# HGRN2 mixer of a four-stage encoder trunk: the value projection as one seven-product 2x2 block product behind four plain gate chunks

## The chip, the cores and the metric

The kernel runs on one core of one Trainium2 chip. The metric is the device time of one execution in microseconds (us); a few executions are taken and their median is given. One more execution is recorded with the hardware profiler, and every row of a profile below comes from such a recording. Time inside the recording is counted from the start of its span.

## What is computed

Two token batches (512 and 256 tokens, 768 in all, 1024 features) go through two macaron layers with shared weights. The first layer's mixer is the one that changes:

```python
# x = x + 0.5 * swiglu_ffn(rmsnorm(x))        for each layer, then the mixer, then a second ffn
def hgrn2_mixer(x, w_in, w_o, g_norm, lb):
    q, i, g, f_fw, f_bw = jnp.split(x @ w_in, 5, axis=-1)     # w_in: [1024, 5*1024]
    f = lb + (1 - lb) * sigmoid(fpre);  k = 1 - f             # per direction
    # S_t = diag(f_t) S_{t-1} + k_t v_t^T,  o_t = S_t^T q_t   forward and backward, v = i
    o = rmsnorm_per_head(o_fwd + o_bwd) * g_norm
    return (o * silu(g)) @ w_o
```

`w_in` has five column ranges of 1024: q, the values i (called v below), g, and the two gate inputs f. There are 8 heads of 128 columns.

## The kernel before, in words

Everything is f32, and each matrix product is taken in three passes on TensorE: every operand is split into a high part (`hi`, a cast to fp32r on ScalarE) and a low part (`lo`, the rest, a subtraction on VectorE), and hi*hi, hi*lo and lo*hi are accumulated in PSUM (`mm3`, L259 to L263). A weight tile needs one cast (L167 or L200 or L266) and one subtraction (L168, L201, L267) before it is used.

The program is written in Python and fully unrolled; a scheduler that ranks instructions by program order, data and free buffers sets the order on each engine. Each engine then runs its own instructions strictly in that order. Buffers come from rings: 8 split weight tiles (`w`), 4 raw weight tiles of 512 KB (`wr`), 2 small raw tiles (`s3`), 8 temporaries (`tA`), 21 large tiles of 6 KB per partition (`big`), 6 token tiles (`x`), 8 PSUM banks (`ps`).

Weights are planned in one queue (`plan`, `plan_quad`) in the order of use. `load_next` issues the DMAs of the next entry on SyncE's queue (SP) when raw tiles are free; `stage_next` splits it into `w` tiles; `take`, `done` and `ahead` keep at most 8 `w` tiles staged.

The feed-forward blocks already use a seven-product scheme: the 2x2 block product of (token halves x feature halves) with (feature halves x column halves) is made with 7 block products in place of 8. Its token factors are b00, b10, b01, b11 (feature half, token half; `block` and `put`) and four sums t1 to t4 of them (`mix`, `sums`, L364 to L379); its weight factors are sums of the four weight blocks, which are made partly by adding DMAs on GpSimd's queue (`into`, L141) and partly on VectorE (L207).

At the end of a feed-forward block, `after_block` normalizes each token block and queues `turn` as deferred work; `turn` (L318) transposes the normalized blocks on TensorE (L331) and copies them out of PSUM. For a feed-forward block the copies go to `tn` (f32) and are split by `put`. For a mixer (row 1 or 4) each copy is split straight out of PSUM into `self.h` (L345 on ScalarE, L346 on VectorE).

The mixer `hgrn` (L832) then runs, in this order: the first half of v's columns for all 768 tokens (`proj_tok("v0")`, 6 blocks of 128 tokens, 24 matmuls of 512 columns each, tokens as the stationary operand); head 0's q and f chunks (`hgrn_proj`, 3 chunks, each 24 matmuls over the 512 tokens and 24 over the 256 tokens, weights stationary); then for each head the scan (`hgrn_scan`, L695: 7 levels of small f32 matmuls at L693, with copies on ScalarE L723 and multiplications on VectorE L745, L749, L751 and predicated copies L712 between the levels), woven with the projection chunks of the next head. The second half of v (`proj_tok("v1")`) is woven into the scan of head 3. After the last scan come g and the output projection.

Of the kernel before, what the change touches and what calls it, by code (L numbers as in the profile page):

```python
# [9 lines left out]
F32 = mybir.dt.float32  # L10
F32R = mybir.dt.float32r
U8 = mybir.dt.uint8
AF = mybir.ActivationFunctionType
# [20 lines left out]
SEQS = ((0, TA), (TA, TB))  # L34
# [8 lines left out]
PACKED = 1  # L43
UP = ("p1", "p7", "p2", "p5", "p4", "p6", "p3")
DOWN = ("p1", "p2", "p5", "p4", "p7", "p6", "p3")
FACTOR = {"p1": "b00", "p2": "b10", "p3": "b11", "p4": "t4", "p5": "t1", "p6": "t2", "p7": "t3"}


class Trunk:
# [94 lines left out]
    def load_next(self):  # L144
        key, srcs, shape, how = self.queue.pop(0)
        raws = []
        for src in srcs:
# [25 lines left out]
    def quad_steps(self, key, raws, srcs, order):  # L173
# [43 lines left out]

        return [(1 if up else 2, lambda name=name: step(name)) for name in order]

    def stage_next(self):  # L220
# [97 lines left out]
    def turn(self, half, part, row, first=False):  # L318
        nc = self.nc
        feeds_ffn = row % 3 != 1  # L320
        if half == 0 and part == 0:
            if feeds_ffn:
                self.ops = {}
                self.tn = {}
            else:
                self.h = [self.big([P, 2, T], F32R) for _ in range(NC)]
# [277 lines left out]
    def proj_tok(self, tag, evac):  # L604
        rest = None
        for gb in range(NBLK):
# [3 lines left out]
            for k in range(NC):  # L610
                key = (tag, k // 2)
                wh, wl = self.take(key)
                a, c = (self.h[k][:, 0, sl], self.h[k][:, 1, sl]), (wh[:, k % 2, :], wl[:, k % 2, :])
                self.mm3(ps, a, c, k == 0, k == NC - 1)
# [43 lines left out]

    def hgrn_proj(self, h, out):
        nc = self.nc  # L660
        qk = self.big([P, 2, T])
        qs, kd = qk[:, 0, :], qk[:, 1, :]
        f, q, k = (self.big([P, 2, T]) for _ in range(3))
        for c0, dst, func in ((0, qs, AF.Copy), (3, f[:, 1, :], AF.Sigmoid), (4, f[:, 0, :], AF.Sigmoid)):
            key = ("hgrn", h, c0)
            wh, wl = self.take(key)
            for s, (off, n) in enumerate(SEQS):
                ps = self.ps(n)
                for kk in range(NC):
                    b = tuple(self.h[kk][:, i, off : off + n] for i in range(2))  # L670
                    self.mm3(ps, (wh[:, kk, :], wl[:, kk, :]), b, kk == 0, kk == NC - 1)
                    if kk in ((1, 3, 5), (3,))[s]:
                        yield
                nc.scalar.activation(dst[:, off : off + n], ps, func)
                if s:
                    self.done(key)
                yield
        for d in range(2):
# [4 lines left out]
        nc.vector.tensor_add(kd, k[:, 0, :], k[:, 1, :])  # L683
        out.update(h=h, qs=qs, kd=kd, f=f, q=q, k=k)

# [122 lines left out]
    def plan_hgrn(self, w_in, w_o):  # L808
        self.plan_tok("v0", w_in, D)
        for h in range(HEADS):  # L810
            for c in (0, 3, 4):
                lo = c * D + h * P
                self.plan(("hgrn", h, c), w_in[:, lo : lo + P], (NC, P))
            if h == 4:
                self.plan_tok("v1", w_in, D + 512)
# [16 lines left out]
    def hgrn(self, lb_row, gn_row, next_row):  # L832
        nc = self.nc
        with self.tc.issue_after(self.last_act), self.tc.issue_after(self.last_dve):
            self.lower_bounds(lb_row)
        self.load_masks()
        self.later(self.spill_x)
        self.hss = self.cp.tile([P, HEADS, NBLK], F32, name="hss")
        vs = {}

        def put_v(half):
            def f(s, b, ps):
                gb = SEQS[s][0] // P + b
                if gb not in vs:
                    vs[gb] = self.xt()
                nc.scalar.copy(vs[gb][:, half * 512 : (half + 1) * 512], ps)

            return f

        self.drain(self.proj_tok("v0", put_v(0)))  # L850
        scan = lambda hd: self.hgrn_scan(hd, vs)
        heads = [{} for _ in range(HEADS)]

        def stream():
            for h in range(1, HEADS):
                yield from self.hgrn_proj(h, heads[h])
                if h == 4:
                    yield from self.proj_tok("v1", put_v(1))

        feed = stream()  # L860
        self.drain(self.hgrn_proj(0, heads[0]))
        lead, early = 4, 2
        for _ in range(lead + early):
            next(feed)
# [453 lines left out]
```

## Time and profile before

| what | us |
|---|---|
| median of 3 runs (2799.24 to 2799.45) | 2799.41 |
| the profiled execution | 2799.13 |
| its span in the trace | 2797.3 |
| last part of the first feed-forward block and first transposes | about 485 to 505 |
| v0, then head 0's chunks | 505 to 576 |
| scans of heads 0 to 7 woven with projections | 576 to 905 |

In the rows below a group reads: line, engine, operation, tile written <- tiles read, shape, xcount, then busy time and mean ns of one, then the engine's idle time just before and who ended it. In timeline rows the two first numbers are start and duration in us; a bracket at the end is idle time before the instruction and what released it. PE is TensorE, PEld its weight loads, DVE VectorE, ACT ScalarE, POOL GpSimd, SP SyncE.

### The profile page before, as it was taken

Reading aid. Unit: us, or ns where it says so; the run is one execution under the profiler, and the core shown is the slowest. Engines: PE = TensorE matmul, PEld = TensorE weight load, DVE = VectorE, ACT = ScalarE, POOL = GpSimd, SP = SyncE. Lnnn points to the kernel's source line nnn. Section 1 sums busy time; section 2 is a strip of 40 time slices with the busy share of each in tenths; the row PEclk is TensorE's granted clock in tenths of the full one; section 3 lists DMA queues with packets and bytes.
Section 4 is the critical chain, followed back from the end, with each engine's and each line's share of the span. In section 5 each row is a group of like instructions: output and inputs, shape, how many; then the busy total and the mean of one; then the engine's idle time right before and its main releaser. Section 6 shows DMA issues by size and latency. Waiting matters only on the chain.

```text
span 2797.3 us, 40580 instructions
## 1 busy us (share of the span) xinstructions
PE 2772.5 (99%) x15225; PEld 2553.0 (91%) x15225; DVE 2159.4 (77%) x3760; ACT 1329.7 (48%) x2455; POOL 369.2 (13%) x402
## 2 busy tenths in 40 slices
PE   8999999999999999999999999999999999999998
PEld 8999999889899889999999999999988889999998
DVE  8788788477577658878878887887858878778877
ACT  7344443444344436444444644444458855444443
POOL 2111121000000001111111111111003211211111
PEclk9999999999999999999999999999999999999999
DMA  6554464311111133555454355545422123655543
GB/s 175 128 129 119 115 144 122 111 46 39 46 40 37 61 98 76 140 133 127 111 128 124 76 137 133 130 111 128 132 72 76 37 61 77 147 133 128 117 115 108
DMA packets 330101, 291.37 MB, mean 104 GB/s; under 512 B 11608, under 2 KB 257840, under 8 KB 329904
## 3 DMA queue, kind: packets, MB, share of 16 engines
q1 hardware_dynamic: 293920, 212.37, 26.1%
q0 software_dynamic: 31680, 62.93, 13.2%
q10 hardware_dynamic: 4304, 13.49, 1.4%
q8 instruction: 119, 1.95, 0.3%
q14 instruction: 78, 0.64, 0.1%
HBM read 216.39 MB, written 9.44 MB: 81 GB/s over the span
## 4 chain that ended last, share of the span: by engine, by line
PE 96%; DVE 2%; ACT 1%; DMA 0%; issue 0%; DVEq 0%; ACTq 0%; SPq 0%
PE ps L437 42%; PE ps L501 20%; PE ps L261 9%; PE ps L263 9%; PE ps L262 9%; PE ps L693 3%; PE ps L797 1%; PE ps L1180 1%; PE ps L773 1%; PE ps L331 1%; PE ps L1142 0%; PE ps L1143 0%; PE ps L1192 0%; PE ps L1193 0%; PE ps L943 0%; DVE x L523 0%
## 5 line engine op out<-in xcount | busy, mean ns | idle before, releaser
L437 PE MATMUL ps<-big,w 128*128 128x384 f32 x6720 | 1169.3, 334 | 0.0
L437 PEld LDWEIGHTS ps<-big,w 128*128 128x128 f32 x6720 | 1165.9, 188 | 1.7 <-ACT tA L454 0.2
L200 ACT CAST w<-wr 128x512 fp32r<-128x512 f32 x600 | 416.1, 706 | 683.5 <-PE ps L437 281.8
L501 PE MATMUL ps<-w,big 128*128 128x512 f32 x2520 | 575.6, 389 | 0.0
L501 PEld LDWEIGHTS ps<-w,big 128*128 128x128 f32 x2520 | 472.7, 188 | 97.8 <-DVE x L523 0.3
L201 DVE TENSOR_TENSOR w<-wr,w 128x512 fp32r<-128x512 f32 (+1 forms) x520 | 430.0, 831 | 155.1 <-ACT w L200 131.2
L523 DVE SCALAR_TENSOR_TENSOR x<-ps,x 128x512 f32<-128x512 f32 x468 | 301.3, 681 | 10.0 <-PE ps L263 9.9
L142 POOL DMA_DIRECT2D s<-wr x120 | 105.0, 875 | 1511.3 <-DMA wr<-in_ffn_w_dram 623.5
L261 PE MATMUL ps<-w,big 128*128 128x512 f32 x624 | 249.0, 399 | 0.5 <-DVE big L1203 0.2
L263 PE MATMUL ps<-w,big 128*128 128x512 f32 x624 | 244.8, 392 | 1.0 <-DVE big L346 1.0
L262 PE MATMUL ps<-w,big 128*128 128x512 f32 x624 | 244.0, 391 | 0.0
L261 PE MATMUL ps<-big,w 128*128 128x384 f32 (+2 forms) x640 | 220.1, 345 | 0.9 <-ACT w L167 0.8
L262 PE MATMUL ps<-big,w 128*128 128x384 f32 (+2 forms) x640 | 216.1, 338 | 0.3 <-DVE big L267 0.2
L263 PE MATMUL ps<-big,w 128*128 128x384 f32 (+2 forms) x640 | 215.2, 336 | 0.0
L266 ACT CAST big<-tA 128x384 fp32r<-128x384 f32 x296 | 148.0, 513 | 114.2 <-DVE tA L476 36.2
L267 DVE TENSOR_TENSOR big<-tA,big 128x384 fp32r<-128x384 f32 x296 | 167.4, 576 | 6.7 <-ACT big L266 4.5
L168 DVE TENSOR_TENSOR w<-wr,w 128x1024 fp32r<-128x1024 f32 x92 | 111.6, 1220 | 75.8 <-ACT w L167 70.4
L201 POOL TENSOR_TENSOR w<-wr,w 128x512 fp32r<-128x512 f32 x80 | 134.0, 1676 | 194.4 <-ACT w L200 193.6
L167 ACT CAST w<-wr 128x1024 fp32r<-128x1024 f32 x92 | 96.5, 1051 | 107.6 <-PE ps L262 85.7
L263 PEld LDWEIGHTS ps<-w,big 128*128 128x128 f32 x624 | 117.2, 188 | 27.1 <-DVE big L346 1.7
L142 POOL DMA_DIRECT2D wr<-wr x100 | 87.7, 877 | 410.5 <-DVE w L201 170.3
L261 PEld LDWEIGHTS ps<-w,big 128*128 128x128 f32 x624 | 117.3, 188 | 23.3 <-issue 1.0
(179 smaller groups left out, 3275.4 us busy)
## 6 DMA issues: line engine op xcount, KB each, us to landing
wr<-in_ffn_w_dram SPq DMA_DIRECT2D x264, 512.0 KB, 4.0
s<-in_ffn_w_dram SPq DMA_DIRECT2D x120, 256.0 KB, 3.3
s<-wr POOLq DMA_DIRECT2D x120, 256.0 KB, 4.9
wr<-wr POOLq DMA_DIRECT2D x80, 256.0 KB, 3.8
wr<-in_hg_w_in_dram SPq DMA_DIRECT2D x40, 512.0 KB, 3.8
wr<-wr POOLq DMA_DIRECT2D x20, 512.0 KB, 4.6
spill<-x ACTq DMA_DIRECT2D x12, 512.0 KB, 3.1
x<-spill ACTq DMA_DIRECT2D x12, 512.0 KB, 3.4
```

Source lines behind the costliest of these rows:

```text
L142: self.nc.gpsimd.dma_start(out, src, accum_op=ALU.add)
L168: self.nc.vector.tensor_sub(lo, raw, hi.bitcast(F32))
L200: nc.scalar.copy(h, src)
L201: (eng or nc.vector).tensor_sub(l, src, h.bitcast(F32))
L261: nc.tensor.matmul(out, a[0], b[0], start=first, stop=False)
L262: nc.tensor.matmul(out, a[0], b[1], start=False, stop=False)
L263: nc.tensor.matmul(out, a[1], b[0], start=False, stop=last)
L266: self.nc.scalar.copy(hi, src)
L267: self.nc.vector.tensor_sub(lo, src, hi.bitcast(F32))
L437: self.nc.tensor.matmul(ps, a[x], b[y], start=first and k == 0 and i == 0, stop=k == 3 and i == 2, skip_group_check=True,)
L501: nc.tensor.matmul(ps, a[x], w[y], start=name == chain and kp == 0 and q == 0, stop=kp == 1 and q == 2, skip_group_check=True,)
L523: self.nc.vector.scalar_tensor_tensor(x, ps, c, x, ALU.mult, ALU.add)
```

## The change

The v projection (both column halves) becomes one block product with 7 in place of 8 block multiplications, right at the start of the mixer but behind four plain chunks (`LEAD`: head 0's q, f forward, f backward, and head 1's q). The chunks are done by token halves of 384: all four for the first half of the tokens, then all four for the second half. The token factors are made as for a feed-forward block (`feeds_ffn = row != 4`), so `self.h` is gone for this mixer, and the projections read the factors b00 to b11. All later chunks are two passes of 384 tokens in place of 512 and 256. v1 is no longer woven into head 3's scan.

```diff
+TOK = ("p1", "p2", "p7", "p6", "p5", "p4", "p3")
+LEAD = ((0, 0), (0, 3), (0, 4), (1, 0))
...
+    def tok_steps(self, key, srcs):
...
+        def fetch(src):
+            t = self.wp.tile([P, 1024], F32, tag="wr", name=self.name("wr"), bufs=RAWBUFS)
+            nc.sync.dma_start(t.rearrange("p (a b) -> p a b", a=2), src[0])
+            parts = [[t], [self.tmp(512), self.tmp(512)]]
+            for a, t in enumerate(parts[1]):
+                self.last_load = nc.sync.dma_start(t, src[1][:, a, :])
+            return parts
+        a11, a12, a21, a22 = (fetch(src) for src in srcs)
+        more = self.big([P, 2, 512])
...
+        for kp in range(2):
+            for a, t in enumerate(s3[kp]):
+                self.last_load = nc.sync.dma_start(t, srcs[2][kp][:, a, :])
+                self.into(t, a11[0][0][:, a * 512 : (a + 1) * 512] if kp == 0 else a11[1][a])
+            for t, u in zip(a21[kp], a22[kp]):
+                self.into(t, u)
+        own = {"p1": a11, "p2": a12, "p3": a12, "p4": a22, "p5": a21, "p6": a11, "p7": s3}
+        sums = {"p6": (a11, a21), "p3": (a12, a11)}
...
-        feeds_ffn = row % 3 != 1
+        feeds_ffn = row != 4
...
-        if half and row % 3 != 1:
+        if half and row != 4:
             self.later(self.sums)
...
+    def tok_quad(self, key, tile):
...
+        for name in TOK:
+            ws = [self.take((*key, name, kp)) for kp in range(2)]
+            chain = {"p2": "p1", "p4": "p5", "p3": "p7"}.get(name, name)
+            for i in range(HB):
...
+                for k in range(4):
...
+                    for q, (x, y) in enumerate(((h, wh), (h, wl), (l, wh))):
+                        nc.tensor.matmul(
...
+                if name == "p1":
+                    nc.scalar.activation(x22, ps, AF.Copy, scale=-1.0)
+                elif name == "p2":
+                    nc.scalar.copy(x11, ps)
+                elif name == "p4":
+                    nc.vector.tensor_add(x21, ps, x22)
+                elif name == "p3":
+                    nc.vector.tensor_sub(x12, ps, x22)
+                elif name == "p5":
+                    nc.vector.tensor_sub(x22, x22, ps)
+                else:
+                    nc.vector.tensor_add(x22, ps, x22)
...
-        self.drain(self.proj_tok("v0", put_v(0)))
+        for half in range(2):
+            for n, (h, c) in enumerate(LEAD):
+                for i, _ in enumerate(self.hgrn_chunk(h, heads[h], c, (half,))):
+                    if half == 0 and n and i != 1:
+                        self.run_later()
+            self.run_later(len(self.deferred))
...
+        for name in self.tok_quad(("v",), vtile):
+            if name == "p6":
+                self.load_masks()
+                self.hgrn_gates(0, heads[0])
...
-            pieces = 18 + 24 * (h == 3) - (lead if h == HEADS - 2 else 0) - (early if h == 0 else 0)
+            pieces = 18 - (2 if h == 0 else 0) - (lead if h == HEADS - 2 else 0)
```

Where instructions stand now is shown at three places. In the rows that follow, numbers behind a name tell buffers apart, and the line is that of the program in question.

TensorE, behind the transposes of the first token half. Before, the first block of v follows: the moving operand (`w`, 512 weight columns) is listed first, the stationary one (`big`, tokens out of `self.h`) second.

```order
L331 MATMUL ps_4678<-ident_r,big_4522 128x128
L331 MATMUL ps_4678<-ident_r,big_4544 128x128
L261 MATMUL ps_4699<-w_4455,big_4594 128x512
L262 MATMUL ps_4699<-w_4456,big_4594 128x512
L263 MATMUL ps_4699<-w_4455,big_4594 128x512
L261 MATMUL ps_4699<-w_4455,big_4595 128x512
```

In the changed program, the same place on TensorE: two plain chunks (banks `ps_4724` and `ps_4751`, weights `w_4455` and `w_4476`, now the stationary operand) begin, with transposes of the second token half between them.

```order
L380 MATMUL ps_4701<-ident_r,big_4540 128x128
L309 MATMUL ps_4724<-big_4611,w_4455 128x384
L309 MATMUL ps_4751<-big_4611,w_4476 128x384
L380 MATMUL ps_4761<-ident_r,big_4562 128x128
L380 MATMUL ps_4761<-ident_r,big_4584 128x128
L380 MATMUL ps_4767<-ident_r,big_4562 128x128
L380 MATMUL ps_4767<-ident_r,big_4584 128x128
L310 MATMUL ps_4724<-big_4611,w_4455 128x384
L311 MATMUL ps_4724<-big_4611,w_4456 128x384
```

`big_4611` is the first half of the factor b00, which `put` writes out of `tn`. The order takes the 12 matmuls of both chunks on b00 before either goes on to b10.

VectorE, ahead of the first scan. Before, one weight of a later chunk (L168), the last gate of head 0 (L683) and the first level's multiplications (L751, L745, L749) stand ahead of the first copy of scores (L707):

```order
L168 TENSOR_TENSOR w_5113<-wr_4924,w_5112 128x1024
L680 TENSOR_SCALAR big_4941<-big_4941,lb_buf 128x768
L682 TENSOR_TENSOR big_4942<-big_4940,big_4941 128x768
L683 TENSOR_TENSOR big_4940<-big_4943 128x768
L751 TENSOR_TENSOR big_5188<-big_4941 128x2x384
L745 TENSOR_TENSOR big_4942<-big_4942,big_4941 128x2x384
L749 TENSOR_TENSOR big_4943<-big_4943,big_4941 128x384 x2
L168 TENSOR_TENSOR w_5182<-wr_4936,w_5181 128x1024
L707 COPY big_5187<-ps_5192 128x512
```

In the changed program the gates and the first level stand further ahead, beside p5 and p4, and right ahead of the first copy of scores (L810) come the weight sums (L255) and splits (L315) of the last product p3, the evacuations of p4 (L743) and p3 (L745), and four weights of later chunks (L173):

```order
L255 TENSOR_TENSOR wr_4645<-wr_4645,wr_4639 128x1024
L743 TENSOR_TENSOR x_5060<-ps_5276,x_5061 128x512
L315 TENSOR_TENSOR w_5320<-wr_4645,w_5319 128x1024
L255 TENSOR_TENSOR tA_4647<-tA_4647,tA_4641 128x512
L743 TENSOR_TENSOR x_5076<-ps_5290,x_5077 128x512
L315 TENSOR_TENSOR w_5326<-tA_4647,w_5325 128x512
L743 TENSOR_TENSOR x_5092<-ps_5304,x_5093 128x512
L745 TENSOR_TENSOR x_5077<-ps_5173,x_5077 128x512
L173 TENSOR_TENSOR w_5430<-wr_5335,w_5429 128x1024
L745 TENSOR_TENSOR x_5093<-ps_5187,x_5093 128x512
L173 TENSOR_TENSOR w_5436<-wr_5337,w_5435 128x1024
L810 COPY big_5441<-ps_5446 128x512
```

(Rows that only repeat one of these with another buffer are left out.) The splits of `w_5430` and `w_5436` need buffers of p3, so they wait for its end.

SyncE's DMA queue, from the first plain weight on. Before, plain weights of 512 KB alone stand there:

```order
L152 DMA wr_4332<-in_hg_w_in_dram 128x2x512
L152 DMA wr_4334<-in_hg_w_in_dram 128x2x512
L152 DMA wr_4378<-in_hg_w_in_dram 128x2x512
L152 DMA wr_4410<-in_hg_w_in_dram 128x2x512
L152 DMA wr_4459<-in_hg_w_in_dram 128x8x128
```

Now the four plain chunks come first, and v's four weight blocks follow, half in raw tiles and half in temporaries, with a third copy of one block (`big_4663`) between them:

```order
L157 DMA wr_4410<-in_hg_w_in_dram 128x8x128
L231 DMA wr_4639<-in_hg_w_in_dram 128x2x512
L234 DMA tA_4641<-in_hg_w_in_dram 128x512
L231 DMA wr_4645<-in_hg_w_in_dram 128x2x512
L234 DMA tA_4660<-in_hg_w_in_dram 128x512
L245 DMA big_4663<-in_hg_w_in_dram 128x512 x2
L231 DMA wr_4651<-in_hg_w_in_dram 128x2x512
L231 DMA wr_4657<-in_hg_w_in_dram 128x2x512
L191 DMA s_1276_8950<-in_ffn_w_dram 128x4x128
```

`wr_4639`, `wr_4645`, `wr_4651` and `wr_4657` are the first halves of the blocks a11, a12, a21 and a22. The program counts 14667 matmuls and transposes on TensorE before and 14631 now; the first 2648 and the last 10006 of them, that is all up to the end of the first feed-forward block and all from behind the last scan on, stand in the same order as before.

More of the change, by code (lines that the diff above doesn't have):

```diff
@@ new lines, in hgrn_chunk @@
+    def hgrn_chunk(self, h, hd, c0, halves):
+        key = ("hgrn", h, c0)
+        wh, wl = self.take(key)
+        if c0 == 0:
+            if "qk" not in hd:
+                hd["qk"] = self.big([P, 2, T])
+            dst, func = hd["qk"][:, 0, :], AF.Copy
+        else:
+            if "f" not in hd:
+                hd["f"] = self.big([P, 2, T])
+            dst, func = hd["f"][:, 4 - c0, :], AF.Sigmoid
+        for half in halves:
+            ps = self.ps(H)
+            for kk in range(NC):
+                b = self.operand(f"b{kk // 4}{half}", kk % 4)
+                self.mm3(ps, (wh[:, kk, :], wl[:, kk, :]), b, kk == 0, kk == NC - 1)
+                if kk in (2, 5):
+                    yield
+            self.nc.scalar.activation(dst[:, half * H : (half + 1) * H], ps, func)
+            if half:
+                self.done(key)
+            yield
@@ L678, in hgrn_proj, with hgrn_gates @@
+    def hgrn_gates(self, h, hd):
+        nc = self.nc
+        qs, kd, f = hd["qk"][:, 0, :], hd["qk"][:, 1, :], hd["f"]
+        q, k = (self.big([P, 2, T]) for _ in range(2))
         for d in range(2):
@@ L683, in hgrn_proj @@
         nc.vector.tensor_add(kd, k[:, 0, :], k[:, 1, :])
-        out.update(h=h, qs=qs, kd=kd, f=f, q=q, k=k)
+        hd.update(h=h, qs=qs, kd=kd, q=q, k=k)
     def halves(self, t, l, par, d):
```

111 lines of the change are left out of this document (70 added, 41 removed).

## The prediction

> **What bounds the kernel now.** First the page: the span, the busy shares, and the shares of the chain of work that ended last.
>
> ```profile
> span 2797.3 us, 40580 instructions
> PE 2772.5 (99%) x15225; PEld 2553.0 (91%) x15225; DVE 2159.4 (77%) x3760; ACT 1329.7 (48%) x2455; POOL 369.2 (13%) x402
> PE 96%; DVE 2%; ACT 1%; DMA 0%; issue 0%; DVEq 0%; ACTq 0%; SPq 0%
> ```
>
> The chain is TensorE, almost throughout. A busy TensorE need not be at its best pace, so the second view is what TensorE waited for in the mixer (485 to 910 us):
>
> ```profile
> PE ps L693 <- ACT big L723: 1.4, 1, 1.4
> PE ps L263 <- DVE big L346: 0.5, 1, 0.5
> ```
>
> Two waits, 1.9 us in 425: the mixer is a stream of matmuls with no hole worth filling. A change here is worth what it does to the number of matmuls times their pace, plus new waits, minus at most these 1.9 us.
>
> The pace is not the mean duration of a group, since matmuls overlap. It is read from the chain in order of time (start, us, what), where a piece ends as the next one starts:
>
> ```profile
> 428.06 28.60 PE ps L501 x126
> 456.66 29.14 PE ps L437 x168
> 615.82 2.68 PE ps L693 x24
> ```
>
> L501 has 512 columns, so 28.60/126 = 0.227 us per matmul; L437 has 384, so 29.14/168 = 0.1735; the scan's 128x128 matmuls take 2.68/24 = 0.112. For 256 columns the timeline gives the start of the 256-token pass of two chunks that follow each other:
>
> ```profile
> 546.66 0.28 PE L261 MATMUL ps<-big,w 128*128 128x256 f32 x1
> 555.00 0.28 PE L261 MATMUL ps<-big,w 128*128 128x256 f32 x1
> ```
>
> 8.34 us for 24 matmuls of 512 and 24 of 256; 24 x 0.227 = 5.45 are the former, so 256 columns take 0.120 each.
>
> **The change part by part. The product:** v0 and v1 are 2 x 6 x 24 = 288 matmuls of 512 columns; seven products of 3 token blocks with 12 each are 7 x 36 = 252. The same form as in `down_quad` (tokens stationary, 512 weight columns), so 0.227 holds: 36 x 0.227 = **8.2 us less** on TensorE. One product is 36 x 0.227 = 8.17 us, the block 57.2.
>
> The Trainium skill, "TensorE: Matmul & The Clock Gate", section "Back-to-back issue gap", gives about 131 ns as the sustained spacing of matmuls with N=512, by which 36 would be worth 4.7 us; the trace has 227 for fp32r operands here, and the trace decides.
>
> **The chunks by halves:** 24 chunks were 24 x 8.34 = 200.2 us; they become 48 passes of 24 matmuls at 0.1735, 199.8. Nothing (0.3 us less).
>
> **The boundary.** Rows of the timeline at the end of the feed-forward block:
>
> ```profile
> 502.58 1.04 ACT L345 ACTIVATE big<-ps,cols 128x384 fp32r<-128x384 f32 x2
> 503.33 1.49 PE L331 MATMUL ps<-ident_r,big 128*128 128x128 f32 x12
> 502.85 1.37 DVE L523 SCALAR_TENSOR_TENSOR x<-ps,x 128x512 f32<-128x512 f32 x2 [1.62 <-PE ps L263]
> 510.48 0.50 PE L263 MATMUL ps<-w,big 128*128 128x512 f32 x1 [0.49 <-DVE big L346]
> ```
>
> And the groups of which the new work is made:
>
> ```profile
> L266 ACT CAST big<-big 128x768 fp32r<-128x768 f32 x60 | 47.2, 846 | 17.3 <-DVE big L370 15.1 <-DVE big L367 2.2
> L267 DVE TENSOR_TENSOR big<-big,big 128x768 fp32r<-128x768 f32 x60 | 54.4, 950 | 8.8 <-ACT big L266 8.8
> L167 ACT CAST w<-wr 128x1024 fp32r<-128x1024 f32 x92 | 96.5, 1051 | 107.6 <-PE ps L262 85.7 <-PE ps L437 20.1 <-DMA wr<-in_ffn_w_dram 1.4
> L168 DVE TENSOR_TENSOR w<-wr,w 128x1024 fp32r<-128x1024 f32 x92 | 111.6, 1220 | 75.8 <-ACT w L167 70.4 <-PE ps L437 4.7
> L311 ACT ACTIVATE big<-x 128x1024 f32<-128x1024 f32 x35 | 37.2, 1065 | 26.8 <-DVE x L521 12.3 <-DVE x L523 11.6 <-DMA x<-in_x_prompt_dram 2.0
> L342 ACT ACTIVATE big<-ps,cols 128x384 f32<-128x384 f32 x56 | 28.6, 595 | 0.5 <-PE ps L331 0.5
> ```
>
> Where ScalarE now writes hi straight out of PSUM (till 503.62 for the first feature half), it copies, then casts 768 columns. Its queue for b10 from 503.62: two casts of b00 (1.7), two weight casts (2.1), the norm of the last block (1.1 and 0.2 for its sum), its root (0.3), four copies (at 0.5, the pace of the row at 502.58), one cast (0.85): 511.9 at full durations, 511.0 where neighbours overlap by a tenth as in these rows. Then 0.95 on VectorE: b10's first half is whole at 512.0 to 512.8. TensorE is free at 504.8 and has till then what the order shows: the 24 matmuls of two chunks on b00 (4.2) and some 18 transposes (2.0), 6.2 us. It idles 0.5 to 1.8 us where before it waited 0.5. I take 1.0, **0.5 us more**. With no cover at all it would stand from 504.8 to 512.8, 8 us: that is the other end.
>
> The second token half goes through the same steps on ScalarE behind the first, 8 copies at 0.5, 4 casts, two evacuations and a table load, from 514 on (the first chunk's end frees its queue): its last low part is done near 525. TensorE comes to it near 525 too: behind 512 it has 26 of its 192 chunk matmuls done, and the 166 left (28.8 us) and 6 transposes end near 541.7, of which the second half is the last 16.7. b01 is done at 519.5, and b11, done at 525, is needed 2 us into a chunk: no wait. From 525 VectorE makes the sums t1 to t4: up to p1's second weight stand 8 subtractions (0.95), 5 splits (0.95) and p1's own (1.22 and two halves):
>
> ```profile
> L201 DVE TENSOR_TENSOR w<-wr,w 128x512 fp32r<-128x512 f32 x400 | 283.3, 713 | 72.7 <-ACT w L200 67.1
> L207 DVE TENSOR_TENSOR wr<-wr,wr 128x1024 f32<-128x1024 f32 x40 | 48.5, 1213 | 0.0
> L207 DVE TENSOR_TENSOR wr<-wr,wr 128x512 f32<-128x512 f32 x80 | 73.7, 921 | 14.8 <-issue 14.0 <-DVE w L201 0.8
> L521 DVE TENSOR_TENSOR x<-ps,x 128x512 f32<-128x512 f32 x48 | 33.0, 688 | 37.8 <-PE ps L263 37.6
> ```
>
> 7.6 + 4.8 + 1.2 + 1.4 = 15.0, so 540, and TensorE needs it at 541.7 + 6 x 0.227 = 543.1. Hidden, with 3 us to spare.
>
> **Weights and DMA.** v takes 5 MB in place of 4 (a21 twice) and seven adding DMAs on POOL. The rows:
>
> ```profile
> 486.31 1.22 DVE L168 TENSOR_TENSOR w<-wr,w 128x1024 fp32r<-128x1024 f32 x1
> 508.62 1.21 DVE L168 TENSOR_TENSOR w<-wr,w 128x1024 fp32r<-128x1024 f32 x1
> wr<-in_ffn_w_dram SPq DMA_DIRECT2D x264, 512.0 KB, 4.0
> s<-wr POOLq DMA_DIRECT2D x120, 256.0 KB, 4.9
> ```
>
> The two L168 rows are the first weight of the mixer and its fourth, at whose place the four chunks' weights are split now: each split frees the raw tile of one of v's blocks. So SP issues the blocks between 488 and 510, and behind the last two loads (4 each) an add (4.9) ends near 525. The small tiles for the sums of p7 come free with the end of the feed-forward block. The first that needs an add is p7, at 541.7 + 16.3 = 558. On SP they stand ahead of the next chunks' weights, which aren't needed before the block ends (599). Cover of over 30 us; nothing. Spilling x and the mask load keep their place on ScalarE's queue.
>
> **Inside the block** each product has 8.17 us of TensorE, against VectorE: 1.22 + 2 x 0.71 for splits, 3 x 0.69 for evacuation, 4.7 us; p6 and p3 add 1.21 + 2 x 0.92 of sums, 7.8. With head 0's gates and first level beside p5 and p4, VectorE is nearly full, and strictly in order. The tightest place is p3's second weight half. Counted from p1's start, p5 ends at 40.9; third evacuation 41.6, sum 42.8, p4's first block (done 43.6) 44.3, split 45.5, sums 47.3, second block 48.0, splits 49.4. TensorE needs it at 49.0 + 1.4 = 50.4. It fits by **1.0 us**. I cost it at nothing; without that cover each us by which VectorE slips further is a us.
>
> **The first scan.** The wait of 1.4 us is here:
>
> ```profile
> 598.42 1.60 PE L693 MATMUL ps<-big,big 128*128 128x128 f32 x12 [1.41 <-ACT big L723]
> 573.00:607.60 34.60, 33.19 (x226) 30.00 (x225) 28.12 (x50) 12.81 (x18) 0.00 (x0) 1.00 0.13 36
> 607.60:649.60 42.00, 42.00 (x294) 38.70 (x293) 33.33 (x59) 18.43 (x34) 0.00 (x0) 1.00 0.14 38
> L712 DVE COPY_PREDICATED big<-big,ps 128x512 f32<-128x512 uint8 x56 | 41.4, 739 | 41.3 <-PE ps L693 41.2
> L712 DVE COPY_PREDICATED big<-big,ps 128x256 f32<-128x256 uint8 x56 | 24.4, 436 | 0.0
> L745 DVE TENSOR_TENSOR big<-big,big 128x768 f32<-128x768 f32 x56 | 53.0, 947 | 23.2 <-ACT big L726 23.2
> L749 DVE TENSOR_TENSOR big<-big,big 128x384 f32<-128x384 f32 x112 | 57.9, 553 | 5.2 <-ACT big L723 1.3
> L723 ACT COPY big<-big 128x768 f32<-128x768 f32 x56 | 50.3, 899 | 91.4 <-PE ps L693 66.7 <-DVE big L749 14.0 <-issue 6.7
> ```
>
> In the windows the numbers are length, then busy PE, PEld, DVE, ACT. Now the gates and the first level are done a product earlier, so the scan starts with operands at hand; but two weight splits wait for p3's buffers and stand ahead of its first copy. VectorE: split 0.9 us after p3's end, evacuation 1.6, split 2.8, then level 0. It meets TensorE at the later levels (some 4.5 us each: 18 matmuls at 0.1735 and 12 at 0.112), against 3.2 us and one short multiplication on VectorE (0.74 + 0.44 + 0.95 + 2 x 0.55) and a copy of 0.9 on ScalarE, with a weight split in every third level. The wait lies between 0.1 us (VectorE catches up before the last levels) and the old 1.4; I take 0.4, nearer the lower end since the old wait fell in the sixth level, beside a split and gates: **1.0 us less**. Heads 1 to 7 keep their 42 us, with VectorE at 33.3 of 42.
>
> **Sum:** 2799.13 - 8.2 - 0.3 + 0.5 - 1.0 = 2790.1 against the profiled execution; the median of the runs lies 0.3 above it: **2790.4**.
>
> **Rivals.** 0.2%, 5.6 us, is about what a measurement of this kernel can tell from no change; the line lies at 2793.8.
>
> *VectorE takes over in and behind the block.* For it: the 1.0 us of cover at p3 and a queue in strict order that waits for buffers. Against it: the other products have 4 to 5 us. With a slip of 3 us p3 waits 2, and the first scan starts behind by the rest and keeps its 1.4 with one wait more: 2790.4 + 2 + 2.4 = 2794.8. Within 0.2%.
>
> *The boundary is not covered.* If the transposes of the second half are held by PSUM banks that ScalarE frees late, more of the 8 us is seen. At 6 of them (5.5 over before): 2795.4. Within.
>
> *A removed matmul is worth less than its pace.* If this stream were held by something other than columns, 36 would be worth as little as the 256-column pace, 36 x 0.120 = 4.3: 2794.3. The 28.60 us row speaks against it: a small chance. The 131 ns of the Trainium skill (the page and section named above) would give nearly the same, 2793.9 by an estimate.
>
> *Slower: the weave of halves leaves VectorE behind in every head.* A pass of 384 gives pieces of 1.56, 1.56 and 1.04 us in place of five nearly equal ones, and the half of v that gave head 3's scan 24 spare pieces is gone. If the small copies at a level's end come late by what the first scan shows (1.4 us), 6 to 7 such waits eat the gain of 9, and from 11 on the kernel is measurably slower; two in each of 7 heads are 14 x 1.4 = 19.6: 2810. Against it: the pieces are the same in sum, and the two windows show 8.7 us of VectorE idle in each head.
>
> That the change doesn't remove what it says is ruled out by the count of matmuls (36 fewer).
>
> **Numbers.** Forecast 0.70; VectorE behind the block 0.11, boundary 0.09, smaller worth 0.03: within 0.2% 0.23; slower 0.07. The range goes from all gains with both old waits gone (2799.4 - 8.5 - 1.9 = 2789.0, and 0.5 for the spread) 2788.5 to past the middle rivals, 2797.
>
> **What would show it.** Right: matmuls of 512 columns at 0.227 in the block; heads at 42 us; waits of TensorE of 1 to 2 us in the mixer. Wrong: a row of TensorE waiting for a `w` split in the block (VectorE), for `big` by L314/L315 ahead of it (the boundary), or a sum of waits behind L826 in heads 1 to 7 (the weave).

## The result and the profile after

The changed kernel takes 2788.51 us (median of 6 runs, 2787.96 to 2788.83) against 2799.51 us for the kernel before in the same comparison (6 runs, 2799.24 to 2799.96): a ratio of 0.996, 95% interval 0.9948 to 0.9973. Its profiled execution took 2788.47 us. It is 11.0 us faster; the forecast was 9.0 us faster (2790.4). The result lies at the very lower end of the range, and taken as a gain, 11.0 us is a little more than the 10.9 that this end allowed from 2799.4. The direction and the largest term were right; the small terms add up to more than the prediction allowed.

The page of the kernel after: span, busy shares, shares of the chain that ended last.

```profile
span 2786.7 us, 40646 instructions
PE 2762.9 (99%) x15189; PEld 2569.4 (92%) x15189; DVE 2191.5 (79%) x3803; ACT 1343.8 (48%) x2479; POOL 376.8 (14%) x409
PE 96%; DVE 2%; ACT 1%; DMA 0%; issue 0%; DVEq 0%; ACTq 0%
```

TensorE has 36 instructions fewer (15225 before) and is as full as it was. VectorE gained 32 us of work, and its share of the chain is 2%, as before. What TensorE itself waited for in the mixer of the kernel after (485 to 910 us), to be held against the two rows that the prediction shows (1.4 and 0.5 us):

```profile
PE ps L796 <- ACT big L826: 0.5, 1, 0.5
PE ps L310 <- DVE big L315: 0.3, 1, 0.3
```

The 1.9 us of waits became 0.8. That isn't enough: 8.2 us of matmuls and 1.1 us of waits make 9.3, not 10.8. The rest is found when the time is cut at the starts of matmuls. In the timeline of TensorE the stretches begin with the first matmul of the last part of the feed-forward block, the first one of a scan (L693 before, L796 after), and the first one of the next feed-forward block. Of the kernel before:

```profile
485.64 0.39 PE L261 MATMUL ps<-w,big 128*128 128x512 f32 x1
574.70 1.60 PE L693 MATMUL ps<-big,big 128*128 128x128 f32 x12
615.65 1.50 PE L693 MATMUL ps<-big,big 128*128 128x128 f32 x12
858.37 1.50 PE L693 MATMUL ps<-big,big 128*128 128x128 f32 x12
900.62 1.50 PE L693 MATMUL ps<-big,big 128*128 128x128 f32 x12
1087.21 1.03 PE L437 MATMUL ps<-big,w 128*128 128x384 f32 x5
```

The same starts in the kernel after, and a row of its chain with the whole block product:

```profile
486.18 0.39 PE L309 MATMUL ps<-w,big 128*128 128x512 f32 x1
599.15 1.50 PE L796 MATMUL ps<-big,big 128*128 128x128 f32 x12
638.71 1.50 PE L796 MATMUL ps<-big,big 128*128 128x128 f32 x12
847.85 1.50 PE L796 MATMUL ps<-big,big 128*128 128x128 f32 x12
890.33 1.50 PE L796 MATMUL ps<-big,big 128*128 128x128 f32 x12
1076.95 1.37 PE L486 MATMUL ps<-big,w 128*128 128x384 f32 x7
```

```profile
542.15 57.16 PE ps L729 x252
```

57.16/252 is 0.2268 us per matmul, so v's 288 took 65.32 before, half of them ahead of the first scan and half in scan 3. Taken out of the stretches, with the four chunks that stand ahead of the first scan (taken as 33.29 us both times, 192 matmuls of 384 columns or the same work in passes of 512 and 256), the account is as follows. Its row for v applies the pace of the kernel after to both kernels; experiment 2 measures that row.

| stretch | before | after | change | forecast |
|---|---|---|---|---|
| v | 65.32 | 57.16 | -8.16 | -8.2 |
| boundary: up to scan 0, without v and four chunks | 23.11 | 22.52 | -0.6 | +0.5 |
| scan 0 | 40.95 | 39.56 | -1.4 | -1.0 |
| scans 1 to 5, without v | 210.06 | 209.14 | -0.9 | 0 |
| scan 6 | 42.25 | 42.48 | +0.2 | 0 |
| scan 7, g, output projection | 186.59 | 186.62 | 0.0 | 0 |
| widths of the chunks | | | 0.0 | -0.3 |
| sum, with the four chunks | 601.57 | 590.77 | -10.8 | -9.0 |

Scan 0 now holds 129 wide matmuls (of 256 columns or more) in place of 120 (0.28 us more work), scan 6 135 in place of 144 (24 of them belong to g, both times; 0.28 us less work); waits and switches alone changed by -1.7 and +0.5 there.

The experiments ask four things: what a removed matmul is worth, which part of the change shortens the scans, whether the boundary had the cover that was claimed for it, and whether VectorE is near to deciding at p3. Differences below some 5 us of the median are not told apart by the runs with certainty; so each verdict rests on the stretch in the trace too. That repeats well: scan 0 has 39.54 to 39.58 us in the seven kernels whose first scan has the order of after.

**Theory A:** 8.2 us are the 36 matmuls at their pace; the other gains are small waits, gone because the pieces of the woven work fall elsewhere. **Theory B:** the block product carries the whole gain, a removed matmul being worth 0.30 us with its weight load.

### The profile page after: what moved, and what is told of

The parts are those of the page before. It is cut to its first block, busy times and chain, and to the rows that moved or that the text cites. A ratio compares the mean times of both kernels' runs of the same rounds, so it can differ in the third digit from the quotient of the medians.

```text
span 2786.7 us, 40646 instructions
## 1 busy us (share of the span) xinstructions
PE 2762.9 (99%) x15189; PEld 2569.4 (92%) x15189; DVE 2191.5 (79%) x3803; ACT 1343.8 (48%) x2479; POOL 376.8 (14%) x409
## 4 chain that ended last, share of the span: by engine, by line
PE 96%; DVE 2%; ACT 1%; DMA 0%; issue 0%; DVEq 0%; ACTq 0%
PE ps L486 42%; PE ps L550 21%; PE ps L310 8%; PE ps L309 8%; PE ps L311 8%; PE ps L796 3%; PE ps L729 2%; PE ps L900 1%; PE ps L1291 1%; PE ps L876 1%; PE ps L380 1%; PE ps L1303 0%; PE ps L1253 0%; PE ps L1254 0%; PE ps L1304 0%; PE ps L1054 0%
## 5 line engine op out<-in xcount | busy, mean ns | idle before, releaser
L486 PE MATMUL ps<-big,w 128*128 128x384 f32 x6720 | 1169.3, 334 | 0.0
L486 PEld LDWEIGHTS ps<-big,w 128*128 128x128 f32 x6720 | 1165.9, 188 | 1.7 <-ACT tA L503 0.2
L550 PE MATMUL ps<-w,big 128*128 128x512 f32 x2520 | 575.3, 389 | 0.0
L550 PEld LDWEIGHTS ps<-w,big 128*128 128x128 f32 x2520 | 472.8, 188 | 97.4
L309 PE MATMUL ps<-big,w 128*128 128x384 f32 x640 | 219.5, 345 | 1.1 <-ACT w L172 1.0
L310 PE MATMUL ps<-big,w 128*128 128x384 f32 x640 | 215.6, 337 | 0.6 <-DVE big L315 0.5
L311 PE MATMUL ps<-big,w 128*128 128x384 f32 x640 | 214.6, 335 | 0.0
L309 PE MATMUL ps<-w,big 128*128 128x512 f32 x528 | 210.9, 399 | 0.3 <-DVE big L1314 0.2
L311 PE MATMUL ps<-w,big 128*128 128x512 f32 x528 | 207.0, 392 | 0.5 <-DVE big L395 0.5
L310 PE MATMUL ps<-w,big 128*128 128x512 f32 x528 | 206.4, 391 | 0.0
L315 DVE TENSOR_TENSOR big<-tA,big 128x384 fp32r<-128x384 f32 x296 | 165.5, 570 | 6.7 <-ACT big L314 4.5
L172 ACT CAST w<-wr 128x1024 fp32r<-128x1024 f32 x84 | 88.2, 1052 | 107.3 <-PE ps L310 78.0
L173 DVE TENSOR_TENSOR w<-wr,w 128x1024 fp32r<-128x1024 f32 x84 | 102.1, 1223 | 41.7 <-ACT w L172 36.7
L212 DVE TENSOR_TENSOR wr<-wr,wr 128x512 f32<-128x512 f32 (+1 forms) x120 | 127.4, 1061 | 6.0 <-issue 5.7
L310 PEld LDWEIGHTS ps<-big,w 128*128 128x128 f32 x640 | 120.5, 188 | 1.9 <-DVE big L315 1.7
## 6 DMA issues: line engine op xcount, KB each, us to landing
wr<-in_ffn_w_dram SPq DMA_DIRECT2D x264, 512.0 KB, 3.9
wr<-in_hg_w_in_dram SPq DMA_DIRECT2D x36, 512.0 KB, 3.7
wr<-wr POOLq DMA_DIRECT2D x21, 512.0 KB, 4.6
spill<-x ACTq DMA_DIRECT2D x12, 512.0 KB, 4.0
x<-spill ACTq DMA_DIRECT2D x12, 512.0 KB, 3.2
```

What stands on the lines that cost most here:

```text
L212: add = {"second": lambda: nc.vector.tensor_add(a11, a11, a21), "fourth": lambda: nc.vector.tensor_add(a12, a12, a11)}
L309: nc.tensor.matmul(out, a[0], b[0], start=first, stop=False)
L310: nc.tensor.matmul(out, a[0], b[1], start=False, stop=False)
L311: nc.tensor.matmul(out, a[1], b[0], start=False, stop=last)
L315: self.nc.vector.tensor_sub(lo, src, hi.bitcast(F32))
L486: self.nc.tensor.matmul(ps, a[x], b[y], start=first and k == 0 and i == 0, stop=k == 3 and i == 2, skip_group_check=True,)
```

## Experiment 1: only the passes of 384, in the kernel before

```diff
-            for s, (off, n) in enumerate(SEQS):
+            for s, (off, n) in enumerate(((0, H), (H, H))):
...
-                    if kk in ((1, 3, 5), (3,))[s]:
+                    if kk in (2, 5):
```

> The kernel before with one part of the change: each chunk of 768 tokens as 384 + 384 in place of 512 + 256. v0 and v1 stay as they were. Theory A (the removed matmuls are worth 0.227 us each, 8.2 in all, and the remaining 2.8 us of the gain are small waits at four places): 0.3 us less by the widths, and 0.17 us less in each woven head, where the copies of the transposed keys (L766 before, L869 after) hold TensorE's weight loads less; 2798.0 us in all (1.5 less), heads 41.83 us apart. Theory B (the whole gain of 10.9 us hangs on the block product, a removed matmul being worth 0.30 us with its weight load): no change, 2799.4, heads 42.00 apart.

Measured: 2797.5 us (11 runs) against 2799.6 of before (21 runs), ratio 0.9993, interval 0.9984 to 1.0001. The first scan's bounds in the timeline of TensorE:

```profile
575.49 1.50 PE L693 MATMUL ps<-big,big 128*128 128x128 f32 x12
615.03 1.50 PE L693 MATMUL ps<-big,big 128*128 128x128 f32 x12
```

Scan 0 takes 39.54 us, as after. Scans 1, 2, 4 and 5 take 41.83 to 41.85 in place of 42.00, scan 6 takes 42.48: again as after. Scan 3, which still holds the second half of v here, keeps its 74.7 us; it gains 0.2 us only in the kernels where that half has gone (after, and experiment 2). From the last part of the feed-forward block to the next one it is 1.9 us less than before. So 1.85 of the scans' 2.1 us come from the passes of 384, with no block product in the kernel. Theory A's sum of 1.5 us came near for a partly wrong reason: the widths gave nothing, and scan 0, which it did not name, gave 1.4. Theory B falls, and so does the reason that the prediction gave for scan 0 (gates and first level done earlier): here they stand where they stood (the last gate starts 4.5 us ahead of the scan, 4.6 before), and scan 0 is as short as in the kernel after, where the gates are done 29 us ahead of it.

## Experiment 2: v as plain matmuls, in the kernel after

```diff
...
-        self.plan_quad(("v",), srcs, None, TOK)
+        self.plan_tok("v0", w_in, D)
+        self.plan_tok("v1", w_in, D + 512)
...
-        for name in self.tok_quad(("v",), vtile):
-            if name == "p6":
-                self.load_masks()
-                self.hgrn_gates(0, heads[0])
...
+        self.drain(self.proj_tok("v0", put_v(0)))
+        self.load_masks()
+        self.hgrn_gates(0, heads[0])
+        self.drain(self.proj_tok("v1", put_v(1)))
```

> The kernel after with v as 288 plain matmuls of 512 columns behind the same four chunks, on the same token factors; the four token sums t1 to t4 are still made, though nothing reads them here. Theory A: 36 matmuls more at 0.227, 8.2 us more than after: 2796.7, unless the change from v0's to v1's weights, which was woven before, adds a wait of up to 1 us (2797.7). Theory B: all of the gain is lost, 2799.3 or more.

Measured: 2796.95 us (11 runs), ratio to before 0.999, interval 0.9981 to 0.9999. First matmul of the stretch, of the first scan and of the next feed-forward block:

```profile
486.66 0.39 PE L309 MATMUL ps<-w,big 128*128 128x512 f32 x1
607.77 1.50 PE L796 MATMUL ps<-big,big 128*128 128x128 f32 x12
1085.64 0.85 PE L486 MATMUL ps<-big,w 128*128 128x384 f32 x4
```

121.11 us against 112.97 after: 8.14 us for 36 matmuls, 0.226 each, and no wait where v0's weights give way to v1's. The rival in which a matmul is worth less than its pace falls with it. The estimate of 4.7 us by the 131 ns of the Trainium skill ("TensorE: Matmul & The Clock Gate", section "Back-to-back issue gap") does not hold for these fp32r matmuls.

The whole stretch takes 598.98 us here against 601.57 before. So 2.6 us are gained by a kernel that still has all 288 matmuls of v.

## Experiment 3: head 0's gates behind the block

```diff
             if name == "p6":
                 self.load_masks()
-                self.hgrn_gates(0, heads[0])
+        self.hgrn_gates(0, heads[0])
```

> The kernel after with head 0's gates written behind the block product in place of beside its sixth product (p6 by the order of the code). Theory A: the gates and first level once more follow close on the scan, VectorE comes late to its later levels, and the 1.4 us wait of before returns at least in part: 1.0 to 1.7 us more than after, 2789.5 to 2790.2, with a wait of L796 for the copies of L826 in the first scan, whose 39.56 us go back towards 40.95. Theory B: the first scan's gain has another source (its passes of 384), and nothing changes: 2788.5, scan 39.6.

Measured: 2788.47 us (5 runs), ratio to before 0.9959, interval 0.9946 to 0.9973. Scan 0 runs from 598.67 to 638.23: 39.56 us, the same. The last gate multiplication of head 0 on VectorE, in the kernel after and in this one:

```profile
569.16 0.95 DVE L785 TENSOR_TENSOR big<-big,big 128x768 f32<-128x768 f32 x1
568.68 0.95 DVE L785 TENSOR_TENSOR big<-big,big 128x768 f32<-128x768 f32 x1
```

The gates have not moved: this kernel's whole stretch lies 0.48 us earlier, and the rows of TensorE, VectorE, ScalarE and GpSimd have the same order, lines and shapes in both traces. The scheduler put the gates where they were. So the edit did not test theory A, and says nothing of where the gates stand; it is experiment 1 that speaks against theory A. What these runs do give is the same order of instructions measured twice: the stretch takes 590.76 and 590.80 us.

## Experiment 4: the leading chunks not by token halves

```diff
-        for half in range(2):
-            for n, (h, c) in enumerate(LEAD):
+        for n, (h, c) in enumerate(LEAD):
+            for half in range(2):
                 for i, _ in enumerate(self.hgrn_chunk(h, heads[h], c, (half,))):
-                    if half == 0 and n and i != 1:
+                    if i != 1:
                         self.run_later()
-            self.run_later(len(self.deferred))
+                self.run_later(len(self.deferred))
```

> The kernel after with the four leading chunks each done for both token halves at once, in place of all four for the first half and then all four for the second. TensorE then has, at the boundary, only one chunk's matmuls on each factor as cover. Theory A (the factors' way over ScalarE and VectorE, up to 8 us, is hidden by the matmuls of the other chunks): TensorE stands about 2 us for b10, 1 for b01, 1.5 for b11, 4.5 us more than after, 2793 (2791.5 to 2794.5). Rival (the factors are ready in time anyhow, since the transposes now go ahead and ScalarE starts the second half earlier): under 1 us more, 2788.5 to 2789.5.

Measured: 2790.41 us (5 runs), ratio to before 0.9967, interval 0.9955 to 0.998: 1.9 more than after, between the two expectations. First matmul of the stretch and of the first scan, and the row where TensorE stands:

```profile
485.87 0.39 PE L309 MATMUL ps<-w,big 128*128 128x512 f32 x1
508.95 2.40 PE L380 MATMUL ps<-ident_r,big 128*128 128x128 f32 x13 [0.50 <-ACT big L391]
600.86 1.50 PE L796 MATMUL ps<-big,big 128*128 128x128 f32 x12
```

114.99 us against 112.97. Doing the chunks by halves is worth 2.0 us in all. It is not the 4.5 of my expectation: the edit also runs the deferred work from the first chunk on, so the second half's transposes go ahead, ScalarE does their eight copies from 511.6 on (from 515.0 in the kernel after), and the factors come earlier. Much of the loss is not a wait for factors either: the transposes (L380) wait for ScalarE's copies (L391), in the row above and for 1.6 us in four waits of the weight loads. So how much a wait for the factors alone would cost is not shown.

## Experiment 5: one piece of woven work moved, in the kernel before

Why do passes of 384 shorten the first scan? In the trace TensorE finds 11 wide matmuls ahead of the sixth level before (2.5 us at their pace), and 21 with the passes of 384 (3.6 us). There VectorE has a long chain before, from a weight split at 590.37 over predicated copies, gates of head 1 and the multiplications of two levels to 597.3. This edit gives the kernel before more there and leaves its widths:

```diff
-    def weave(main, feed, pieces, steps=LEVELS + 1):
+    def weave(main, feed, pieces, early=None, steps=LEVELS + 1):
...
-            while used * steps < (i + 1) * pieces:
+            while (used - (i == early)) * steps < (i + 1) * pieces:
...
-            self.weave(scan(heads[h]), feed, pieces)
+            self.weave(scan(heads[h]), feed, pieces, 4 if h == 0 else None)
```

> The kernel before, with one piece of the woven chunks moved in the first scan: three pieces in place of two ahead of the sixth level, one in place of two ahead of the seventh (23 wide matmuls in place of 11, then 12 in place of 24; the same work in all). Theory A (the 1.4 us wait of the first scan is a matter of how much matmul work stands where VectorE's chain is longest; the passes of 384 help only because they put 21 matmuls there): the wait goes, the first scan takes 39.5 us in place of 40.95, 2798.0 in all; up to 0.5 more if the seventh level now waits. Rival (passes of 384 as such are cheaper or come to ScalarE at a better time): the scan keeps 40.9 us, 2799.4.

Measured: 2798.58 us (11 runs) against 2799.52 of before (15 runs), ratio 0.9996, interval 0.9987 to 1.0005. The first scan's bounds, and the waits of TensorE in the mixer:

```profile
575.39 1.60 PE L693 MATMUL ps<-big,big 128*128 128x128 f32 x12
615.34 1.50 PE L693 MATMUL ps<-big,big 128*128 128x128 f32 x12
```

```profile
PE ps L263 <- DVE big L346: 0.5, 1, 0.5
PE ps L693 <- DVE big L745: 0.2, 1, 0.2
```

The wait of 1.4 us is gone and a smaller one of 0.2 has come at the next level. Scan 0 takes 39.95 us, within what theory A expected (39.5, and up to 0.5 more with a wait at the seventh level) and 1.0 less than before with the same work; the whole stretch is 0.9 us shorter. The passes of 384 give 1.4, and 1.7 when the 0.28 us of work that they add to this scan is counted. So 1.0 of 1.7 us is a matter of where the pieces fall. Of the other 0.7 us, some 0.2 is the new wait here and 0.17 what the passes give scans 1, 2, 4 and 5 too; the rest is not placed.

## Experiments 6 and 7: more work on VectorE ahead of p3

```diff
+            if name == "p3" and kp == 0:
+                t = sums[name][0][kp][0]
+                for _ in range(2):
+                    self.tc.keep_in_program_order(nc.vector.tensor_max(t, t, t))
             if name in sums:
```

The second has `range(4)`.

> The kernel after with two more VectorE instructions of p3's first weight sum (a maximum of a tile with itself, which changes nothing), about 2.3 us, ahead of that sum. By the trace of after p3's second weight is split at 590.58 and needed at 592.5, and VectorE stands 0.9 us for p4's first block on the way there: 2.8 us of cover, no wait, 2788.5. By the 1.0 us of cover that the prediction worked out: 1.3 us more, 2789.8.

> The same with four more such instructions, about 4.6 us. With 2.8 us of cover TensorE waits 1.8 us at p3 and nothing more behind it, since the first scan's chain starts with p3's own end: 2790.3. By the prediction's rival, in which the first scan starts behind as well: 3.6 us of wait at p3 and up to 2.4 behind it, 2792.1 to 2794.5.

Measured: 2788.91 and 2789.05 us (5 runs each), both with a ratio to before of 0.9962, interval 0.9949 to 0.9974. From the last part of one feed-forward block to the next block it is 0.1 and 0.4 us more than after. With two instructions the expectation of no wait held, just: p3's second weight is split at 593.28 in place of 590.58, 2.7 us later, and by the starts of its matmuls TensorE loses less than 0.1 us there. So the cover at p3 is about 2.6 us. With four, of 1.22 us each, none of the forecasts held: neither 1.8 nor 3.6 us of wait is there. The timeline of TensorE in the second of these kernels shows why (L733 is the block product, L800 the scan):

```profile
587.77 2.88 PE L733 MATMUL ps<-w,big 128*128 128x512 f32 x12
590.49 1.27 PE L800 MATMUL ps<-big,big 128*128 128x128 f32 x10
591.53 0.96 PE L733 MATMUL ps<-w,big 128*128 128x512 f32 x3
592.33 0.38 PE L800 MATMUL ps<-big,big 128*128 128x128 f32 x2
592.54 0.39 PE L800 MATMUL ps<-big 128*128 128x128 f32 x2
592.79 7.96 PE L733 MATMUL ps<-w,big 128*128 128x512 f32 x33
```

The scheduler set 14 of the 24 matmuls of the scan's first level (L800) into the place where p3 would have had to wait. The order is not fixed while VectorE slips: this slip was written into the program, and the scheduler filled it. What p3 would cost beyond its cover with the order held fast was not tried and stays open.

## Experiment 8: the same shift in the kernel after

Scan 6 has in the kernel after a wait that before did not have, at its last level:

```profile
873.25 1.60 PE L796 MATMUL ps<-big,big 128*128 128x128 f32 x12 [0.48 <-ACT big L826]
```

The edit is that of experiment 5, with `5 if h == HEADS - 2 else None`.

> The kernel after with one piece moved in the scan of head 6: three pieces in place of two ahead of its last level, one in place of two behind it (24 wide matmuls in place of 15, then 9 in place of 18). Theory A (as in the first scan of before, the wait lies where too little matmul work stands beside VectorE's longest chain): the 0.5 us wait of L796 in this scan goes, its 42.48 us become 41.8 to 42.0, 2787.9 in all. Rival (the wait only moves on to the transposes behind the last level): 2788.5.

Measured: 2787.72 us (5 runs), ratio to before 0.9958, interval 0.9945 to 0.997. The bounds of scan 6, and all that TensorE still waits for in the mixer:

```profile
847.35 1.50 PE L796 MATMUL ps<-big,big 128*128 128x128 f32 x12
889.05 1.50 PE L796 MATMUL ps<-big,big 128*128 128x128 f32 x12
```

```profile
PE ps L310 <- DVE big L315: 0.3, 1, 0.3
```

41.70 us in place of 42.48; the wait is gone and has not moved on. This version has the lowest time of all kernels here, 0.8 us below after in the median and 0.7 in the whole stretch of the trace. A gain of that size shows in the stretch; by the medians alone it could not be claimed.

## Why the prediction was right or wrong

**The matmuls: right.** 8.2 us forecast and 8.14 measured in experiment 2. The pace read from the chain was the price; the mean duration of the group, 0.39 us, would have given 14.

**The bound of 1.9 us: wrong, and this is the step that failed.** The prediction said "minus at most these 1.9 us", and set the low end of its range by it. Without the matmuls the kernel gained 2.6 us (experiment 2 shows the same 2.6 with all matmuls in place). Against the forecast of 9.0 the 10.8 us of the stretch are 1.8 more: the boundary gave 1.1 us more than its term, scans 1 to 5 gave 0.9 where nothing was put down, and scan 0 gave 0.4 more; scan 6 and the widths took back 0.5. The view of TensorE's waits lists idle time of the matmuls alone. Time is lost too where a weight load waits and the next matmul starts late, though the row of the matmul before it still covers the gap. That has rows under PEld, which I did not read. The two longest before, 485 to 910 us:

```profile
PEld ps L773 <- ACT big L766: 2.3, 7, 0.5
PEld ps L693 <- ACT big L723: 2.0, 2, 1.8
```

And after:

```profile
PEld ps L876 <- ACT big L869: 1.6, 6, 0.3
PEld ps L796 <- ACT big L826: 1.0, 2, 0.8
```

The first row of each is the end of the scans: the weight loads of L773 (L876) wait for the copied keys. 2.3 us in seven waits became 1.6 in six. These waits overlap with work that goes on, so they are not a price; the price is read from the starts.

**"Heads 1 to 7 keep their 42 us": wrong by some 0.2 in each of scans 1 to 5.** The timelines at the end of scan 1, before and after:

```profile
649.64 0.48 PE L261 MATMUL ps<-big,w 128*128 128x512 f32 x1
650.12 1.16 PE L773 MATMUL ps<-x,big 128*128 128x128 f32 x8
651.58 1.05 PE L773 MATMUL ps<-x,big 128*128 128x128 f32 x8
```

```profile
673.33 0.33 PE L309 MATMUL ps<-big,w 128*128 128x384 f32 x1
673.61 2.05 PE L876 MATMUL ps<-x,big 128*128 128x128 f32 x16
```

Before, one wide matmul stands between the transposes of the keys and L773, and the group is torn in two; after, four stand there (by the trace), and the group is whole. The first L773 comes 0.48 us behind that wide matmul in place of 0.227, so 0.25 us is lost (0.08 of it by the change to a wide matmul, see the last section), and after it is 0.28 in place of 0.17, so 0.11: TensorE's waits show neither. Yet the end of the scan explains only a part of scan 1's 0.17: from the keys' transposes to the next scan it takes 8.80 us before with 12 wide matmuls, and 8.61 after with 15; less their work at the paces of the prediction, 6.08 and 6.01. Where the rest lies is not shown. That the passes of 384 do it in scans 1, 2, 4 and 5 is shown by experiment 1. The slower rival (the weave of halves leaves VectorE behind) did not come: five of the six woven scans behind the first gained, and scan 6 lost 0.2. Its count was off as well: before, a chunk had six nearly equal pieces (four of 1.36 us and two of 1.44), not five.

**The first scan: size nearly right (-1.4 for -1.0), cause wrong.** It was put down to gates and first level done a product earlier. Experiment 1 has the whole gain with the gates where they were (39.54 us, and 39.56 with the gates early), so they add nothing to the passes of 384. The 1.4 us stall is a matter of how much matmul work lies beside VectorE's chain (experiment 5). I had compared means, 4.5 us of TensorE's work per level against VectorE's, where the pieces between two levels differ: 11, 12, 13 or 24 matmuls before.

**The boundary: mis-sized, +0.5 forecast and -0.6 measured.** Two things. Before, TensorE lost more than the 0.5 us of the waits view: by the starts, the transpose at 509.72 is followed only at 510.48 by a matmul (0.73 us lost), and 0.38 goes at 504.55 behind twelve transposes. After, the one gap is at the first low part of b00:

```profile
506.57 0.44 PE L310 MATMUL ps<-big,w 128*128 128x384 f32 x1 [0.32 <-DVE big L315]
```

by the starts 0.56 us. So the loss went from 1.1 to 0.56 us, where the prediction had 0.5 and 1.0. And the place that I priced, b10, costs nothing. ScalarE's first cast of b10, VectorE's two subtractions for its low part and the first matmul that needs one of them, in the kernel after:

```profile
510.49 0.87 ACT L314 CAST big<-big 128x768 fp32r<-128x768 f32 x1
511.39 1.83 DVE L315 TENSOR_TENSOR big<-big,big 128x768 fp32r<-128x768 f32 x2 [0.72 <-ACT big L314]
512.40 0.44 PE L310 MATMUL ps<-big,w 128*128 128x384 f32 x1
```

The time that I gave for b10's first half, 512.0 to 512.8, was right: its low part is done at about 512.3. But TensorE needs it later than I had it. Held up by the 0.56 us at b00, it is busy till 511.86, and its first matmuls on b10 (L309, at 511.86 and 512.12) need only the high part, which is there at 511.36. It comes to the low part at 512.40. The rival of a boundary without cover did not come; by experiment 4 the arrangement by halves is worth 2.0 us, not up to 8. That the 0.6 us lie at these gaps is read from the starts and was not tried by itself.

**The cover at p3: too small in the prediction.** It was worked out as 1.0 us for both halves of p3's second weight. VectorE in the kernel after:

```profile
589.29 1.29 DVE L315 TENSOR_TENSOR w<-tA,w 128x512 fp32r<-128x512 f32 x2
```

Both halves are done at 590.58, and p3 (which starts at 591.0) needs the first of them 1.4 us later, at 592.3: at least 1.8 us, and experiment 6 shows about 2.6. That it costs nothing was right, and the rival of VectorE behind the block did not come about; nor did it with four more instructions of 1.22 us (experiment 7), where the scheduler filled the place.

**Weights and DMA, and widths:** no wait of TensorE for a `w` split is listed in the block, as forecast. The 0.3 us by the widths was rounding: 0.227 and 0.120 make twice 0.1735.

## What to carry to other kernels

A change in the number of matmuls on a full TensorE was worth their start-to-start pace; that term came out to a tenth of a microsecond. What is left to gain besides is bounded by the starts of the matmuls against their pace, stretch by stretch, with the weight loads' waits read as well; the waits of the matmuls alone show too little. Where small dependent steps are woven with bulk work, count the bulk between each two steps against the other engine's chain at that very step: moving one piece took out 1.0 us in one scan and 0.8 in another. And where a scheduler sets the order, see in the trace that an edit has moved what it was to move: the edit of experiment 3 moved nothing, and that of experiment 7 moved more than was meant.

## What the runs showed of the hardware beside this

A change from 128-column matmuls to wide ones shifts the starts and costs almost nothing. Behind the first level of scan 0 of the kernel after:

```profile
601.75 0.42 PE L309 MATMUL ps<-big,w 128*128 128x384 f32 x1
602.00 0.33 PE L310 MATMUL ps<-big,w 128*128 128x384 f32 x1
602.17 0.34 PE L311 MATMUL ps<-big,w 128*128 128x384 f32 x1
```

The first wide matmul starts 0.03 us behind the last small one in place of 0.11, and the second starts 0.25 behind the first in place of 0.17. The same 0.03 and 0.31 in place of 0.227 stand in the kernel before for 512 columns. A small matmul behind a wide one starts at the wide one's pace (0.17 us). Together it is under 0.01 us per change, so the number of changes in a scan (20 before, 18 after, in scans 0 and 1) is not what was gained.
